# Mixture-of-experts layer on one core: four expert-weight loads under way instead of two, and a block's token slots dealt to the 16 DMA engines in turn

## The chip, the cores and the metric

The kernel runs on one core of one Trainium2 chip. The metric is the device time of one execution in microseconds (us). Work is done by TensorE (PE in the profile, its weight loads PEld), VectorE (DVE), ScalarE (ACT) and GpSimd (POOL). SyncE (SP) issues the plain loads, GpSimd issues the indirect ones, and 16 DMA engines move the data of both.

## The reference, cut to what matters

One layer of a generator is computed for 512 latent tokens of width 1024: two token mixers, then a mixture of experts, then a norm. The change touches the mixture alone.

```python
scores = jax.nn.sigmoid(jnp.matmul(h, w_router, preferred_element_type=jnp.float32))
_, idx = lax.top_k(scores + b_router.astype(jnp.float32), TOP_K)      # 8 of 64 experts a token
wts = jnp.take_along_axis(scores, idx, axis=-1)
wts = (wts / jnp.sum(wts, -1, keepdims=True) * ROUTE_SCALE).astype(h.dtype)
...
def expert_block(acc, blk):
    tok, wt, e = blk
    yb = swiglu(h_pad[tok], w_e_gate[e], w_e_up[e], w_e_down[e]) * wt[:, None]
    return acc.at[tok].add(yb), None
...
return swiglu(h, w_sh_gate, w_sh_up, w_sh_down) + routed[:n]
```

512 tokens with 8 experts each make 4096 (token, expert) pairs. The gate, up and down matrices of an expert are 1024 x 256, 1024 x 256 and 256 x 1024, all float32.

## The kernel before

The mixers, the output projection, the router and the hidden layer of the shared expert fill the first 560 us or so. Then come the experts, in `experts` (L1354), and last a norm of the sum in `tail` (L1558).

**Blocks.** The experts are ranked by their token counts (`rank`), and the rank decides how many slots an expert gets: `CAPS` for the 34 that have a block of 128 partitions to themselves (128, 112, 96 or 80 slots), `PCAPS` for the 30 that share a block two by two (64, 48 or 32 slots, in partitions 0 to 63 and 64 to 127). One more block holds what two large experts have beyond 128. With the two experts of that block, the slots add up to 5376, over 66 slot ranges in 50 blocks. `ORDER` sets the blocks' order: first four single ones, then mostly one pair and two singles in turn, four singles at the end.

**Tables.** For each slot range, `tables` (L1136) compares a row of running numbers (`iot`) with each token's place in its expert's list (`posm`). The result is a one-hot matrix `oh` (four chunks of 128 tokens by 128 slots), and matmuls with it give each slot its token's index and weight. Slot p holds the expert's token number p, so the unused slots are the last ones of the range. An unused slot gets an index out of bounds, whose row is neither read nor written. The tables are made in the background (`background`, L1345), a few blocks ahead of their use.

**A step.** `run` (L1409) works off one block. `fetch` (L1310) gathers the tokens' rows of 4 KB from DRAM by an indirect DMA (`xg<-h2d`), `xpose` turns them, `prep` (L1220) splits each quarter of the weights in two terms (ScalarE writes the first one, VectorE the second, tile `gq`), `mm` multiplies, `act` and `ph` make the hidden layer, `py` (L1279) multiplies by the down matrix. Then an indirect DMA with addition adds the rows into the sum `accd` in DRAM (L1306). A pair has two gathers and two such additions. Since all additions go to one tensor, each waits until the one before has landed. GpSimd issues gathers and additions, in its program order, between multiplications by a gate (L1300).

**Loads of weights.** Each expert has three loads of 1 MB (gate and up in two, down in one) into one of 13 tiles `rw` (`NR`). SP issues them in one order; `pump` issues the next when a tile's last reader has been recorded. `load_part` (L1179) adds one more wait: a load waits until the load `DQ` before it has landed.

```python
self.under_way.append(ins)
if len(self.under_way) > self.DQ:
    self.tc.add_manual_dep(ins.ins, self.under_way[-1 - self.DQ].ins.name, ...
```

There are 195 such loads: 64 experts and the shared one, three each.

Of the kernel before, what the change touches and what calls it, by code (L numbers as in the profile page):

```python
# [12 lines left out]
ALU = mybir.AluOpType  # L13
# [4 lines left out]
P = 128  # L18
# [10 lines left out]
GTYPE = (0, 1, 1, 2)  # L29
NE = 64  # L30
FF = 256

VC_C, VC_CC, VC_NG, VC_ADA = 0, 8, 16, 24
VC_U, VC_TQK, VC_NQ, VC_NK, VC_GA, VC_GB, VC_N = 40, 48, 49, 53, 57, 65, 73
# [39 lines left out]
class Kern:  # L74

    NR, GQ, XB, YB, LQ = 13, 4, 2, 3, 3

    FA, DQ = 2, 2

    TBG, TBN = (1, 2, 4), 12  # L80

# [918 lines left out]
    def shared(self):  # L1000
# [3 lines left out]
        for k in range(KB):  # L1004
            raw = self.raw["sh", k // 4][1].rearrange("p (k f) -> p k f", k=4)[:, k % 4, :]
            w = p1.tile([P, 2, 2 * FF], F32R, name="shw", tag="wlo", bufs=2)
            self.split(w[:, 0, :], w[:, 1, :], raw)
# [4 lines left out]
        for tag in ("sw", f"vals{NE}"):  # L1012
            h = mid.tile([P, 2, FF], F32, name="hs", tag=tag)
            self.hs += [h[:, i, :] for i in range(2)]
        for pg, h in zip(pgs, self.hs):
            sg = p1.tile([P, FF], F32, name="sgs", tag="sgt", bufs=2)
            nc.scalar.activation(sg, pg[:, :FF], AF.Silu)
            nc.vector.tensor_tensor(h, sg, pg[:, FF:], op=ALU.mult)
        self.slots += [self.raw.pop(("sh", n))[0] for n in range(2)]
# [116 lines left out]
    def tables(self, blocks, posm, vals, ps=None):  # L1136

        nc, p2 = self.nc, self.p2
        n = len(blocks)
        pool, tag = (p2, "oh") if ps is None else (self.p1, "sgt")  # L1140
        if ps is None:
            ps = self.ps2.tile([P, n, 6], F32, name="ptab", tag="tab", bufs=1)
        for i, block in enumerate(blocks):
            oh = pool.tile([P, 4, P], BF, name="oh", tag=tag, bufs=2)
            m = P // len(block)
            for p0, (r, t0, _) in zip((0, m), block):
                nc.vector.tensor_tensor(oh[:, :, p0:p0 + m], self.iot[:, None, t0:t0 + m].to_broadcast([P, 4, m]),  # L1147
                                        posm[:, :, r:r + 1].to_broadcast([P, 4, m]), op=ALU.is_equal)
            for b in range(4):
                for p0, (r, _, _) in zip((0, m), block):  # L1150
                    nc.tensor.matmul(ps[p0:p0 + m, i, :], lhsT=oh[:, b, p0:p0 + m], rhs=vals[:, b, r, :],  # L1151
                                     start=b == 0, stop=b == 3)
            yield
        ix, w = self.finish_table(p2 if pool is p2 else self.mid, ps, n)

        half = ix
        if any(len(block) > 1 for block in blocks):
            half = p2.tile([P // 2, n], I32, name="half", tag="half", bufs=self.NTB)
            nc.vector.tensor_copy(half, ix[P // 2:])
        self.tb += [([t[:, i:i + 1] for t in (ix, half)], w[:, i:i + 1]) for i in range(n)]  # L1160
        yield
# [7 lines left out]
    def early(self):  # L1169

        p2 = self.p2
        raw = lambda r: [([P, 2048], F32, f"r{i}") for i in r]
        gq = lambda r: [([P, 2, 2, 2 * FF], F32R, f"gq{i}") for i in r]
        xg = lambda r: [([P, D], F32, f"xg{i}") for i in r]
# [509 lines left out]
```

## Time and profile before

| | us |
|---|---|
| median of three runs | 1391.91 |
| lowest and highest run | 1390.16, 1394.66 |
| the profiled execution, its own time | 1389.76 |
| its span, first to last instruction | 1388.0 |
| PE, DVE, ACT, POOL busy | 1216.1, 905.2, 664.4, 397.8 |

The profiled execution is 1.8 us longer than its span and 2.2 us below the median. Busy times are unions over the whole span; a matmul's own time contains its way through the array, so back-to-back matmuls overlap, and a busy PE may still have room. The DMA share is the time that packets took on the 16 engines; it tells that a packet was under way, not at what speed.

### The profile page before, as it was taken

What the parts mean: (1) busy time and instruction counts of PE and PEld (TensorE: products, weight loads), DVE (VectorE), ACT (ScalarE), POOL (GpSimd) and SP (SyncE); (2) the same over time, 40 slices, a digit from 0 to 9 for tenths busy, and PEclk for the clock granted to TensorE, in tenths of its full rate; (3) what the DMA queues carried; (4) which work ended last, traced back from release to release, by engine and by line L of the source; (5) the groups of instructions that cost most, each with busy time, mean ns of one, the idle gap of its engine ahead of it and who ended that gap; (6) DMA issues with size and microseconds to landing.
All of it is one profiled execution on the core that took longest, in us unless ns stands there. A gap on an engine that the chain in (4) does not pass through costs nothing. (4 is left out here: it accounts for less than half of the span.)

```text
span 1388.0 us, 18578 instructions
## 1 busy us (share of the span) xinstructions
PE 1216.1 (88%) x6305; PEld 862.1 (62%) x6305; DVE 905.2 (65%) x1535; ACT 664.4 (48%) x1146; POOL 397.8 (29%) x374
## 2 busy tenths in 40 slices
PE   6999999999999999898868998787887879777992
PEld 4866887877777788676535555555554546444661
DVE  4536357577687756779958787666665756565653
ACT  4312253365555533355536665555465545454651
POOL 2301103411211000336334343333342333242342
PEclk9999999999999999999988999999998999988996
DMA  9999436655675365857988999999999999999995
GB/s 326 308 295 294 138 114 147 195 141 128 140 155 115 115 211 182 290 201 262 309 276 252 320 296 312 313 306 317 314 313 313 301 330 304 304 327 308 313 328 149
DMA packets 106171, 349.18 MB, mean 252 GB/s; under 512 B 13809, under 2 KB 41050, under 8 KB 81114
## 3 DMA queue, kind: packets, MB, share of 16 engines
q1 hardware_dynamic: 82058, 287.89, 61.0%
q0 software_dynamic: 23552, 58.49, 18.9%
q10 hardware_dynamic: 464, 1.59, 0.3%
q8 instruction: 51, 0.84, 0.2%
q14 instruction: 46, 0.38, 0.1%
HBM read 321.03 MB, written 37.44 MB: 258 GB/s over the span
## 5 line engine op out<-in xcount | busy, mean ns | idle before, releaser
L1229 DVE TENSOR_TENSOR gq<-rw,gq 128x1024 fp32r<-128x1024 f32 x258 | 321.0, 1256 | 132.0 <-ACT gq L1227 130.9
L1243 PE MATMUL pg<-gq,xx 128*128 128x512 f32 x1328 | 401.5, 439 | 3.1 <-DVE gq L1229 1.7
L1227 ACT CAST gq<-rw 128x1024 fp32r<-128x1024 f32 x264 | 273.3, 1046 | 144.8 <-DMA rw<-in_w_exp_dram 91.4
L1243 PEld LDWEIGHTS pg<-gq,xx 128*128 128x128 f32 x1328 | 248.2, 198 | 97.8 <-issue 43.9
L1287 PE MATMUL py<-rw,hT 128*128 128x512 f32 (+1 forms) x560 | 220.1, 633 | 45.0 <-DMA rw<-in_w_exp_dram 41.0
L1287 PEld LDWEIGHTS py<-rw,hT 128*128 128x128 f32 (+1 forms) x560 | 76.4, 175 | 129.7 <-issue 116.8
L1300 POOL TENSOR_TENSOR y<-y,gf 128x512 f32<-128x512 f32 x52 | 82.1, 1579 | 226.9 <-ACT y L1299 226.7
L96 ACT CAST whi<-raw 128x1024 fp32r<-128x1024 f32 (+1 forms) x60 | 61.4, 1023 | 130.4 <-PE mmp L114 43.6
L97 DVE TENSOR_TENSOR wlo<-raw,whi 128x1024 fp32r<-128x1024 f32 (+1 forms) x60 | 71.3, 1189 | 74.9 <-ACT whi L96 74.9
L1306 POOL DMA_INDIRECT accd<-y,ix x50 | 84.5, 1691 | 113.5 <-DVE gq L1229 27.7
L113 PE MATMUL mmp<-hhi,whi 128*128 128x512 f32 x256 | 103.8, 406 | 0.0
L115 PE MATMUL mmp<-hhi,wlo 128*128 128x512 f32 x256 | 101.1, 396 | 0.0
L114 PE MATMUL mmp<-hlo,whi 128*128 128x512 f32 x256 | 100.8, 394 | 0.0
L1319 POOL DMA_INDIRECT xg<-h2d,ix x50 | 58.0, 1161 | 82.3 <-PE xt L1331 51.3
L1331 PE MATMUL xt<-ident,xg 128*128 128x128 f32 x400 | 63.3, 284 | 16.5 <-DMA xg<-h2d,half 15.6
L97 DVE TENSOR_TENSOR xx<-xt,xx 128x512 fp32r<-128x512 f32 x100 | 68.2, 683 | 13.6 <-ACT xx L96 13.2
L1331 PEld LDWEIGHTS xt<-ident,xg 128*128 128x128 f32 x400 | 51.2, 148 | 28.0 <-issue 18.9
L96 ACT CAST xx<-xt 128x512 fp32r<-128x512 f32 x100 | 58.2, 583 | 16.1 <-PE xt L1331 15.3
L762 POOL DMA_DIRECT2D q<-qdr x32 | 17.7, 555 | 144.5 <-PE stp L809 141.9
L1147 DVE TENSOR_TENSOR oh<-iot,posm 128x512 bf16<-128x512 f32 (+1 forms) x66 | 53.3, 835 | 8.2 <-PE ptab L1151 8.2
L1302 DVE SCALAR_TENSOR_TENSOR y<-py,tw,gf 128x512 f32<-128x512 f32 x52 | 38.8, 745 | 30.1 <-PE py L1287 23.7
L113 PEld LDWEIGHTS mmp<-hhi,whi 128*128 128x128 f32 x256 | 48.2, 188 | 12.5 <-issue 3.0
(416 smaller groups left out, 2097.5 us busy)
## 6 DMA issues: line engine op xcount, KB each, us to landing
rw<-in_w_exp_dram SPq DMA_DIRECT2D x195, 1024.0 KB
raw<-in_w_in_dram SPq DMA_DIRECT2D x40, 512.0 KB
araw<-in_w_ada_dram SPq DMA_DIRECT2D x64, 256.0 KB
araw<-in_w_ada_dram SPq DMA_DIRECT2D x16, 512.0 KB
k<-kdr POOLq DMA_DIRECT2D x32, 192.0 KB, 6.1
nab<-in_nab_dram SPq DMA_DIRECT2D x24, 256.0 KB
x<-in_x_dram SPq DMA_DIRECT2D x8, 512.0 KB
q<-qdr POOLq DMA_DIRECT2D x32, 128.0 KB, 5.2
```

The source lines that it names most:

```text
L96: self.nc.scalar.copy(hi, src)
L97: (eng or self.nc.vector).tensor_tensor(lo, src, self.r32(hi), op=ALU.subtract)
L113: mm(ps, lhsT=ahi, rhs=bhi, start=first, stop=False)
L114: mm(ps, lhsT=ahi, rhs=blo, start=False, stop=False)
L115: mm(ps, lhsT=alo, rhs=bhi, start=False, stop=last)
L1227: nc.scalar.copy(t[:, 0, :, sl], src)
L1229: eng.tensor_tensor(t[:, 1, :, sl], src, self.r32(t[:, 0, :, sl]), op=ALU.subtract)
L1243: nc.tensor.matmul(pg, lhsT=st.x[:, q * 2 + k, a, :], rhs=t[:, b, k, :], start=q + k + n == 0, stop=q + k + n == 3 + len(terms))
L1287: nc.tensor.matmul(py[s], lhsT=st.hT[:, j, s], rhs=d[:, j * D + c * 512:j * D + c * 512 + 512], start=j == 0, stop=j == 1)
L1300: nc.gpsimd.tensor_tensor(o, o, gf, op=ALU.mult)
L1306: nc.gpsimd.indirect_dma_start(out=self.accd[:], out_offset=bass.IndirectOffsetOnAxis(ap=ix[:cap], axis=0), in_=y, in_offset=None, bounds_ ...
L1331: self.nc.tensor.transpose(tp[:, k * P:k * P + P], st.xg[:, (q * 4 + k) * P:(q * 4 + k + 1) * P], self.ident)
```

## The change

`DQ` goes from 2 to 4: a weight load now waits for the landing of the fourth load before it. And the slots of a range are filled in another order. With cap slots and k = cap / 16, slot q*k + i holds the expert's token number i*16 + q: sixteen runs of k neighbouring slots, and the tokens are dealt to the runs in turn. Slots beyond the cap, in a block whose range is shorter than its room, are filled by a second comparison.

```diff
+NQ = 16
...
-    FA, DQ = 2, 2
+    FA, DQ = 2, 4
...
-            for p0, (r, t0, _) in zip((0, m), block):
-                nc.vector.tensor_tensor(oh[:, :, p0:p0 + m], self.iot[:, None, t0:t0 + m].to_broadcast([P, 4, m]),
-                                        posm[:, :, r:r + 1].to_broadcast([P, 4, m]), op=ALU.is_equal)
+            for p0, (r, t0, cap) in zip((0, m), block):
+
+                k = cap // NQ
+                nc.vector.tensor_tensor(oh[:, :, p0:p0 + cap].rearrange("p b (q i) -> p b q i", q=NQ),
+                                        self.iot[:, None, t0:t0 + cap].rearrange("p b (i q) -> p b q i", q=NQ)
+                                        .to_broadcast([P, 4, NQ, k]),
+                                        posm[:, :, r:r + 1, None].to_broadcast([P, 4, NQ, k]), op=ALU.is_equal)
+                if cap < m:
+                    nc.vector.tensor_tensor(oh[:, :, p0 + cap:p0 + m],
+                                            self.iot[:, None, t0 + cap:t0 + m].to_broadcast([P, 4, m - cap]),
+                                            posm[:, :, r:r + 1].to_broadcast([P, 4, m - cap]), op=ALU.is_equal)
```

Gathers and additions keep their number and their lists of cap slots. The orders of PE, POOL and SP are the same as before, row for row, but for the waits. On SP, in the middle of the expert loads, four loads stood like this before (the loads raise the semaphores DMAHW0 to DMAHW7 in turn; a load that waits for DMAHW5 raises DMAHW7; the second wait is for the tile's last reader):

```order
L1181 DMA rw_7718<-in_w_exp_dram 128x2048 [waits DMAHW5_49,DVE_49]
L1181 ISA
L1181 DMA rw_7743<-in_w_exp_dram 128x2048 [waits DMAHW6_49,DVE_49]
L1181 ISA
L1181 DMA rw_7781<-in_w_exp_dram 128x2048 [waits DMAHW7_49,DVE_49]
```

The same place on SP now:

```order
L1190 DMA rw_7726<-in_w_exp_dram 128x2048 [waits DMAHW3_49,DVE_49]
L1190 ISA
L1190 DMA rw_7751<-in_w_exp_dram 128x2048 [waits DMAHW4_49,DVE_49]
L1190 ISA
L1190 DMA rw_7789<-in_w_exp_dram 128x2048 [waits DMAHW5_49,DVE_49]
```

Each load waits for a semaphore two places further back; the wait for the tile's reader stays.

On VectorE, among the tables of the first group of eight blocks, there stood before:

```order
L1229 TENSOR_TENSOR gq<-rw,gq 128x1024
L1147 TENSOR_TENSOR oh<-iot,posm_6297 128x512
L1147 TENSOR_TENSOR oh<-iot,posm_6297 128x4x64 x2
L1229 TENSOR_TENSOR gq<-rw,gq 128x1024
L1302 SCALAR_TENSOR_TENSOR y<-py,tw,gf 128x512
```

The same place on VectorE now:

```order
L1238 TENSOR_TENSOR gq<-rw,gq 128x1024
L1150 TENSOR_TENSOR oh<-iot,posm_6297 128x4x112
L1155 TENSOR_TENSOR oh<-iot,posm_6297 128x4x16
L1150 TENSOR_TENSOR oh<-iot,posm_6297 128x4x64 x2
L1238 TENSOR_TENSOR gq<-rw,gq 128x1024
```

A range of 112 slots, which was one comparison over 128, is now one over 112 and one over 16. In all, 66 comparisons become 103: 66 over the caps and 37 over the rest.

## Rows read from the trace of the kernel before

**Rows 1.** The page: span, busy time by engine, and DMA share in 40 slices.

```profile
span 1388.0 us, 18578 instructions
PE 1216.1 (88%) x6305; PEld 862.1 (62%) x6305; DVE 905.2 (65%) x1535; ACT 664.4 (48%) x1146; POOL 397.8 (29%) x374
DMA  9999436655675365857988999999999999999995
```

**Rows 2.** Stretches: length, PE, PEld, DVE, ACT, POOL busy, then clock, DMA share, GB/s.

```profile
560.00:650.00 90.00, 77.53 (x429) 59.32 (x428) 70.61 (x159) 42.14 (x76) 37.50 (x29) 0.94 0.71 245
650.00:1350.00 700.00, 581.83 (x2463) 367.57 (x2461) 478.50 (x568) 377.90 (x519) 257.15 (x176) 0.92 0.96 307
1350.00:1388.00 38.00, 10.60 (x33) 5.50 (x32) 14.33 (x22) 6.08 (x14) 11.51 (x12) 0.70 0.55 170
```

**Rows 3.** Waits of the engines, 650 to 1350: us in total, times, longest.

```profile
ACT gq L1227 <- DMA rw<-in_w_exp_dram: 91.4, 40, 6.2
POOL accd L1306 <- DMA accd<-y,ix: 66.7, 18, 7.9
...
PE py L1287 <- DMA rw<-in_w_exp_dram: 41.0, 7, 7.7
...
POOL accd L1306 <- DMA accd<-y,half: 23.5, 5, 5.3
```

**Rows 4.** Waits of SP's queue, 650 to 1350, the same columns.

```profile
SPq L1181 <- DMA rw<-in_w_exp_dram: 524.1, 170, 7.7
SPq L1181 <- DVE gq L1229: 14.8, 13, 4.0
```

**Rows 5.** DMA, 650 to 1350: packets; queues (packets, MB, share); issues (count, size, us to landing).

```profile
DMA packets 37234, 215.03 MB, mean 307 GB/s; under 512 B 6980, under 2 KB 6980, under 8 KB 15038
q1 hardware_dynamic: 24920, 181.50, 73.3%
q0 software_dynamic: 12272, 33.03, 22.0%
...
rw<-in_w_exp_dram SPq DMA_DIRECT2D x173, 1024.0 KB
accd<-y,ix POOLq DMA_INDIRECT x46, 9.2
xg<-h2d,ix POOLq DMA_INDIRECT x45, 9.5
...
accd<-y,half POOLq DMA_INDIRECT x16, 7.7
xg<-h2d,half POOLq DMA_INDIRECT x15, 10.5
accd<-y,rows POOLq DMA_INDIRECT x3, 8.7
```

**Rows 6.** DMA, 1235 to 1236.4, weight loads alone.

```profile
DMA packets 74, 0.57 MB, mean 404 GB/s; under 512 B 5, under 2 KB 5, under 8 KB 5
q1 hardware_dynamic: 74, 0.57, 97.6%
```

**Rows 7.** DMA, 1238 to 1239, during an addition into accd.

```profile
q0 software_dynamic: 34, 0.14, 75.3%
q1 hardware_dynamic: 9, 0.06, 13.7%
```

**Rows 8.** POOL's timeline, 912 to 928: start, us, instruction, idle before and releaser.

```profile
912.84 1.61 POOL L1306 DMA_INDIRECT accd<-y,ix  x1 [3.29 <-DMA accd<-y,half]
...
925.50 1.57 POOL L1306 DMA_INDIRECT accd<-y,ix  x1 [7.87 <-DMA accd<-y,ix]
```

**Rows 9.** The comparisons of L1147: ns min/median/max, first and last start, forms.

```profile
L1147 DVE TENSOR_TENSOR oh<-iot,posm x66: 403/678/3075, 596.1 to 1078.7; 128x512 bf16<-128x512 f32 x34, 128x256 bf16<-128x256 f32 x32
```

**Rows 10.** VectorE's timeline at 649: one of its small instructions.

```profile
649.00 0.15 DVE L1129 TENSOR_TENSOR ta<-tb 128x2 f32<-128x2 f32 x1
```

**Rows 11.** VectorE's busy time in L1147 alone, 650 to 700.

```profile
650.00:700.00 50.00, 18.99 (x21) 0.97 0.95 306
```

**Rows 12.** VectorE's busy time as a whole, 650 to 700.

```profile
650.00:700.00 50.00, 49.23 (x70) 0.97 0.95 306
```

## Prediction

> **What bounds the kernel now.** The page comes first [rows 1]: PE is busy for 88% of the span, which looks like the bound, but the DMA share stands at 9 tenths nearly throughout the second half. So the stretches come next [rows 2]. From 650 to 1350, half of the span and nearly all of the expert steps, the DMA share is 0.96, PE is busy for only 582 of 700 us, VectorE for 479, ScalarE for 378. From 560 to 650, and after 1350, the DMA engines have room. The change can act on the 700 us.
>
> What the engines wait for there [rows 3]: ScalarE for weights 91.4 us, PE for down matrices 41.0 us. Those 132 us are paid by compute. Why weights come late is read from SP's own queue [rows 4]: of 700 us it waits 524.1 us, 170 times, for the landing of an earlier load, and only 14.8 us for VectorE to give a tile back. So a free tile is nearly always there, and what holds the next load back is the wait on the load two before it.
>
> Then the question is whether the DMA engines could take more, as 0.96 says that they are full. One load moves 1024 KB in packets of 8 KB, 8 for each engine. With weights alone under way, 69 such packets (74 less the 5 small ones) took 97.6% of 16 engines for 1.4 us, 317 ns each, at 404 GB/s [rows 6]. Over the 700 us, 181.50 MB are 22,156 packets of 8 KB, and 73.3% of 16 x 700 us makes 371 ns each, at 307 GB/s with everything [rows 5]. So the share holds 54 ns in each packet that a fed engine doesn't need. And within an addition into accd [rows 7], weights have only 13.7% of the engines, 2 of 16, while the additions have 75.3%, 12 of 16: most engines have done their parts of both loads under way and have no more weights to move until the slowest engine has finished and the next load has come. The 0.96 is not all work.
>
> **The work of the slowest engine.** Weights: 173 loads x 8 packets x 317 ns = 439 us for each engine. The gathers and additions: 15,038 - 6,980 = 8,058 packets of 4 KB [rows 5], 22.0% of 16 x 700 us = 2,464 us of engine time, 306 ns each. 3 of the 125 indirect DMAs carry all 128 rows, so the other 122 carry (8,058 - 384) / 122 = 62.9 rows. Their ranges have 5,376 / 66 = 81.5 slots. If an engine takes cap / 16 neighbouring slots, an engine with early slots has 81.5 / 16 = 5.1 rows each time and one with the last slots none. The front engine's sum: 122 x 5.1 + 3 x 8 = 646 rows, 198 us, in all 637 us. It is at work for 91% of the 700 us, and 63 us are its dry spells.
>
> **The change, part by part.**
>
> *Dealt slots.* Every engine gets 62.9 / 16 = 3.9 rows, rounded up on the front engine, 4.4 on the average: 122 x 4.4 + 24 = 561 rows, 172 us. The slowest engine's work falls to 439 + 172 = 611 us, 26 us less. With no rounding it would be 593 us. If the runs of slots aren't what an engine gets, this part gives 0; no row here tells which engine moves which slot.
>
> *Four under way.* It adds no transfer, it only puts the issue two landings earlier. A load lasts at least 8 x 317 ns = 2.5 us; with two more queued an engine can be 5 us ahead of the slowest and still have weights. Two bounds: all 63 us of dry spells go, or none. Some will stay, since SP's other waits will show up once this one is short: with 13 tiles and four under way, the wait for VectorE, 14.8 us now [rows 4], takes over whenever compute is the slower. I take half, 32 us.
>
> *One-hots.* 66 comparisons of the same elements in all become 103. The 37 more are priced from below by a small instruction, 0.15 us [rows 10], and from above by the shortest half-width comparison, 0.40 us [rows 9]: 6 to 15 us of VectorE. The first operand is now read with steps of 16 elements; no row shows that. The bounds are nothing, and twice the time, 19 us more in 650 to 700 [rows 11]. VectorE is hidden by the DMA wait later (479 of 700 us), but not in 650 to 700, where it is busy for 49.2 of 50 us [rows 12] and feeds the tables that gathers wait for. A third of the comparisons falls there (21 of 66), so some 12 of the 37, 2 to 5 us. I take 3 us, with no price for the steps, and keep 0 to 24.
>
> *What becomes next.* PE's 582 us, VectorE's 479 and the chain of additions. That chain: 46 x 9.2 + 16 x 7.7 + 3 x 8.7 = 573 us from issue to landing [rows 5], each waiting for the one before, as [rows 8] shows in the 7.87 us before 925.50. GpSimd's waits on it are 90 us so far [rows 3]. With 65 x 0.3 us between them it is 592 us, the nearest to 611. So several bounds lie near 600, and a stage with several of them doesn't reach the lowest: another reason for half.
>
> **The sum.** 700 - 26 - 32 + 3 = 645 us for the stretch. The span goes from 1388.0 to 1333 us. With 1.8 us around it, 1334.8; the profiled execution was 2.2 us below the median of the runs shown, so about 1337.
>
> A page has a bound of its own. The Trainium skill, DMA: Bandwidth & Descriptors, section Bandwidth, puts the share of one core in the memory's rate at about 358 GB/s and the fabric at 435. By the first figure the 215.03 MB of the stretch would take at least 601 us, an estimate that leaves the sum as it is; the 404 GB/s over 1.4 us [rows 6] show that the first is no limit for a moment, and no run here shows it for longer.
>
> **The rivals.**
>
> 1. *Packets are slow for another reason.* If the 54 ns are lost in the memory or between two queues on one engine, not in dry spells, the engines are full at 0.96, and only 4% of 700 us, 28 us, is to be had, and dealing out rows takes nothing off. For it: a share of 0.96. Against it: [rows 7]. Half of the 28 us, less the 3 us of comparisons, gives 1381, all of them 1367; I say 1372.
>
> 2. *The slots don't sit in runs.* Then the front engine stays as it is, 637 us plus half of the dry spells is 669, plus 3 us 672: 28 us less, about 1364. Beside it stands a rule: the same page, section The descriptor swizzle, gives each engine of a direct transfer two groups of four partitions, 32 apart. No row shows whether gathers and additions follow it.
>
> 3. *The additions become the bound, and it is slower.* With weights always queued, an addition's row of 354 ns (75.3% of 16 us over 34 packets [rows 7]) has to wait for weight packets of 317 ns on its engine. One a row adds 4.4 x 317 ns = 1.4 us, less 0.7 x 354 ns = 0.2 us for the rows saved: the chain is 592 + 65 x 1.2 = 670 us, and the time at best 1362. With two weight packets for each row it is 592 + 65 x 2.6 = 761 us, 61 us more than now: 1453. It decides from 1.7 us an addition, a median landing of 10.9 us for `accd<-y,ix`. Against it: landings of 9.2 us hold competition already. Beside it stands the page's rule, section Queues, rings and completion order, that an engine takes its queues in turn, packet by packet; that is the lighter case.
>
> 4. *SP is held by tiles instead.* Free tiles now come early [rows 4], but if compute's own order (PE's 582 us) sets the pace, nothing is won beyond small change: 1390.
>
> **Chances.** The forecast 0.56, rival 1 0.18, rival 2 0.10, rival 3 0.09 (half of it in the lighter case), rival 4 0.07. The forecast's own range is 1290 (all dry spells gone and most of the rounding, 598 us) to 1376 (none gone, 26 us less, and 10 us more for the comparisons). The lower end of the whole, 1285, is 593 us for the stretch with the comparisons hidden. The upper end, 1385, takes in rivals 1 and 2 and leaves out rival 4 and the heavy case of 3. 0.3% is 4 us, about the distance between the lowest and the highest run. Faster by more than that: 0.55 + 0.15 + 0.09 + 0.04 = 0.83. Within it: 0.09, most of rival 4 and the weak end of rival 1. Slower: 0.08, the heavy case of rival 3 and comparisons that cost more than twice.
>
> **What would show it.** Right: SP's wait for landings falls from 524 us to below 300, and its waits for VectorE, PE or ScalarE rise; ScalarE's and PE's waits for weights fall from 132 us to below 50; the GB/s of the stretch rise to 330 or more; the mean of an 8 KB packet falls towards 317 ns, or the weights keep their share during an addition. The landing of `accd<-y,ix` stays within 8 to 10 us. If it rises beyond 11 us and GpSimd's waits on accd grow by more than those on weights fall, rival 3 holds. If SP's wait is short, the share is 0.97 and the GB/s are unchanged, it is rival 1. L1150 with L1155 should add 6 to 15 us; 50 us would show that the steps are paid. What makes the prediction wrong above all is that I take half of the dry spells with no row for how the remaining waits add up.

## The result, and the profile after

| | us |
|---|---|
| before, median of four runs (lowest, highest) | 1391.11 (1390.16, 1394.66) |
| changed, median of four runs (lowest, highest) | 1353.98 (1347.73, 1361.02) |
| ratio, 95% interval | 0.973 (0.968 to 0.978) |
| forecast | 1337 (1285 to 1385) |
| profiled execution of the changed kernel, its span | 1361.02, 1359.2 |

Faster by 37 us, where the sum had 55 (26 + 32 - 3). The profiled execution is the slowest of the four, 7 us above the median, and its stretches are longer by that in all. The weights' loads end earlier, and the stretch that was 650 to 1350 is now about 650 to 1320.

The stretches of the changed kernel, columns as in [rows 2]:

```profile
560.00:650.00 90.00, 77.25 (x398) 59.26 (x398) 67.45 (x141) 39.02 (x72) 34.04 (x28) 0.89 0.67 236
650.00:1320.00 670.00, 575.95 (x2487) 368.50 (x2486) 498.33 (x624) 381.41 (x523) 263.55 (x179) 0.94 0.95 325
1320.00:1359.00 39.00, 13.69 (x46) 7.91 (x44) 13.38 (x22) 6.93 (x15) 11.99 (x12) 0.72 0.44 129
```

307 GB/s have become 325, but the DMA share is as high as before: the share alone could not tell that there was room. SP's queue, 650 to 1320 (us, times, longest), answers to [rows 4]:

```profile
SPq L1190 <- DVE gq L1238: 200.3, 61, 8.4
SPq L1190 <- DMA rw<-in_w_exp_dram: 141.0, 75, 4.9
SPq L1190 <- PE py L1296: 90.0, 30, 13.0
SPq L1190 <- DVE hh L1277: 55.3, 15, 17.2
```

The wait for earlier landings fell from 524 to 141 us; SP now waits mostly for tiles that compute has not given back. The other engines in the same stretch, against [rows 3]: what they wait for, and in the last line what is left of the weights. Three waits of the kernel before that [rows 3] leaves out, 650 to 1350, stand ahead of them.

```profile
POOL accd L1306 <- DVE gq L1229: 31.5, 9, 5.2
...
PE ptab L1151 <- DVE oh L1147: 18.5, 8, 9.3
...
PE xt L1331 <- DMA xg<-h2d,half: 15.6, 5, 6.0
```

```profile
POOL accd L1315 <- DMA accd<-y,ix: 65.4, 18, 7.8
...
POOL accd L1315 <- DVE gq L1238: 41.9, 10, 6.8
...
PE xt L1340 <- DMA xg<-h2d,half: 35.5, 9, 7.8
...
POOL accd L1315 <- DMA accd<-y,half: 31.8, 6, 6.7
...
PE ptab L1160 <- DVE oh L1155: 20.3, 9, 13.3
...
ACT gq L1236 <- DMA rw<-in_w_exp_dram: 2.5, 2, 1.7
```

Of 132 us of waits for weights 2.5 are left. PE waits longer for the gather of a pair's second half (35.5 us, 15.6 before). Its 20.3 us for the second comparisons of L1155 are hardly new: the comparisons of L1147 held it for 18.5 us before. The DMA of the stretch, against [rows 5]:

```profile
DMA packets 37769, 217.88 MB, mean 325 GB/s; under 512 B 7066, under 2 KB 7066, under 8 KB 15326
...
q1 hardware_dynamic: 25344, 184.04, 72.1%
q0 software_dynamic: 12382, 33.33, 22.7%
...
accd<-y,ix POOLq DMA_INDIRECT x47, 9.1
...
accd<-y,half POOLq DMA_INDIRECT x16, 8.3
accd<-y,rows POOLq DMA_INDIRECT x3, 8.9
```

The landing of an addition has hardly grown: 9.2 us before and 9.1 now under `ix` (single blocks and the first halves of pairs), 7.7 and 8.3 under `half` (the second halves). The comparisons, 560 to 1359 (busy us, mean ns), beside [rows 9]:

```profile
L1150 DVE TENSOR_TENSOR oh<-iot,posm 128x256 bf16<-128x256 f32 (+6 forms) x66 | 52.0, 800 | 14.3 <-PE ptab L1160 14.3
L1155 DVE TENSOR_TENSOR oh<-iot,posm 128x64 bf16<-128x64 f32 (+2 forms) x37 | 16.4, 444 | 0.0
```

How a late gather comes about, on GpSimd's timeline, 1055 to 1090 (start, us, instruction, idle before it and releaser), and then on PE's:

```profile
1070.43 1.50 POOL L1315 DMA_INDIRECT accd<-y,ix  x1 [6.80 <-DVE gq L1238]
1072.23 1.31 POOL L1328 DMA_INDIRECT xg<-h2d,ix  x1 [0.30 <-DVE oh L1155]
1073.85 1.73 POOL L1328 DMA_INDIRECT xg<-h2d,half  x1 [0.30 <-issue]
1075.88 0.96 POOL L1328 DMA_INDIRECT xg<-h2d,ix  x1 [0.30 <-issue]
```

```profile
1085.00 1.08 PE L1340 MATMUL xt<-ident,xg 128*128 128x128 f32 x4 [4.89 <-DMA xg<-h2d,half]
```

GpSimd stands idle for 6.80 us ahead of an addition; three gathers are queued behind it in GpSimd's order and go out one after the other when it is released; the pair's second half, issued at 1073.85, lets PE start at 1085.00, after 4.89 us of waiting. The profile names VectorE as the releaser. The trace says otherwise: the addition before, issued at 1060.33, landed 9.3 us later, at 1069.6, 0.8 us ahead of this start. All ten additions that the profile puts down to `gq` start 0.78 to 0.81 us after the landing of the one before, as the six named for a half's landing do (0.76 to 0.81); the eighteen named for a landing under `ix` start after 0.27 to 0.82 us. The run `two_acc` below bears it out.

### The profile page after: what moved, and what is told of

It is laid out like the page before. It is cut to its first block, busy times and chain, and to the rows that moved or that the text cites. A ratio compares the mean times of both kernels' runs of the same rounds, so it can differ in the third digit from the quotient of the medians.

```text
span 1359.2 us, 18614 instructions
## 1 busy us (share of the span) xinstructions
PE 1212.7 (89%) x6305; PEld 864.5 (64%) x6305; DVE 921.3 (68%) x1572; ACT 665.2 (49%) x1146; POOL 400.8 (29%) x374
## 5 line engine op out<-in xcount | busy, mean ns | idle before, releaser
L1238 DVE TENSOR_TENSOR gq<-rw,gq 128x1024 fp32r<-128x1024 f32 x258 | 326.5, 1278 | 75.8 <-ACT gq L1236 74.8
L1296 PE MATMUL py<-rw,hT 128*128 128x512 f32 (+1 forms) x560 | 207.5, 605 | 4.6 <-ACT hT L1286 2.5
L1315 POOL DMA_INDIRECT accd<-y,ix x50 | 85.9, 1719 | 145.9 <-DVE gq L1238 41.9
L1296 PEld LDWEIGHTS py<-rw,hT 128*128 128x128 f32 (+1 forms) x560 | 72.3, 167 | 84.6 <-issue 67.6
L1309 POOL TENSOR_TENSOR y<-y,gf 128x512 f32<-128x512 f32 x52 | 78.7, 1514 | 146.9 <-ACT y L1308 146.5
L1340 PE MATMUL xt<-ident,xg 128*128 128x128 f32 x400 | 65.4, 290 | 36.1 <-DMA xg<-h2d,half 35.5
L1150 DVE TENSOR_TENSOR oh<-iot,posm 128x256 bf16<-128x256 f32 (+6 forms) x66 | 52.0, 800 | 14.3 <-PE ptab L1160 14.3
L116 PEld LDWEIGHTS mmp<-hhi,wlo 128*128 128x128 f32 x256 | 48.1, 188 | 10.7 <-issue 0.8
```

What stands on the lines that cost most here:

```text
L116: mm(ps, lhsT=alo, rhs=bhi, start=False, stop=last)
L1238: eng.tensor_tensor(t[:, 1, :, sl], src, self.r32(t[:, 0, :, sl]), op=ALU.subtract)
L1296: nc.tensor.matmul(py[s], lhsT=st.hT[:, j, s], rhs=d[:, j * D + c * 512:j * D + c * 512 + 512], start=j == 0, stop=j == 1)
L1309: nc.gpsimd.tensor_tensor(o, o, gf, op=ALU.mult)
L1315: nc.gpsimd.indirect_dma_start(out=self.accd[:], out_offset=bass.IndirectOffsetOnAxis(ap=ix[:cap], axis=0), in_=y, in_offset=None, bounds_ ...
L1340: self.nc.tensor.transpose(tp[:, k * P:k * P + P], st.xg[:, (q * 4 + k) * P:(q * 4 + k + 1) * P], self.ident)
```

## The experiments

Ratios are to the kernel before, run in the same job; that kernel's median was 1390 to 1396 us in the jobs.

**Each part alone, and more loads.**

`dq4_only` leaves the slots as before, `deal_only` the loads, and `dq8` is the changed kernel with eight loads under way:

```diff
-    FA, DQ = 2, 2
+    FA, DQ = 2, 4      # dq4_only, from the kernel before
-    FA, DQ = 2, 4
+    FA, DQ = 2, 2      # deal_only, from the changed kernel
-    FA, DQ = 2, 4
+    FA, DQ = 2, 8      # dq8, from the changed kernel
```

> Four loads under way, slots as before. By the forecast's sum (the front engine's 637 us of work stay, half of 63 us of dry spells go) it is about 1360 us, 30 us faster than before, and the weights' waits of ScalarE and PE fall as in the changed kernel. If dealing the slots gives nothing, it is the changed kernel's 1354 us or a little less, since it saves 37 comparisons. If the slowest engine sets the pace whatever is queued, it is within 10 us of before (1391 us).

> Dealt slots, two loads under way as before. By the forecast (26 us off the front engine, 3 us for comparisons) about 1368 us. If an engine doesn't get a run of k neighbouring slots, nothing is gained and the comparisons cost 0 to 5 us: 1391 to 1396 us. The first of an addition's 16 landings should come later than before and the last one earlier or the same.

> The changed kernel with eight loads under way. If compute and its tiles are now the bound (SP's waits there are 200 us for VectorE and 90 us for PE beside 141 us for landings), it is within 8 us of the changed kernel's 1354 us. If dry spells remain, it is 10 to 30 us faster. If queued weights slow the gathers and additions, their landings pass 10 us and it is slower than 1360 us.

| | median us | ratio (95%) |
|---|---|---|
| dq4_only | 1361.22 | 0.9735 (0.9695 to 0.9775) |
| deal_only | 1386.76 | 0.9943 (0.9909 to 0.9976) |
| dq8 | 1351.71 | 0.9694 (0.9649 to 0.9740) |

SP's first rows, 650 to 1300, of `dq4_only`, `deal_only` and `dq8`:

```profile
SPq L1181 <- DMA rw<-in_w_exp_dram: 212.6, 87, 4.8
SPq L1181 <- DVE gq L1229: 162.8, 57, 9.9
```

```profile
SPq L1190 <- DMA rw<-in_w_exp_dram: 456.0, 149, 6.2
SPq L1190 <- DVE gq L1238: 27.5, 18, 4.4
```

```profile
SPq L1190 <- DVE gq L1238: 295.5, 72, 13.5
SPq L1190 <- PE py L1296: 89.1, 33, 7.3
SPq L1190 <- DVE hh L1277: 73.6, 14, 16.6
```

Four loads under way alone give as much as both changes, 37 us by the ratio (31 to 43) and 34 between the medians. The dealing alone gives 8 (3 to 13). On top of the four loads it shows nothing (0.973 against 0.9735), but that difference is known to some 9 us only, so 0 and 8 are not told apart. With eight, SP waits for no landing of a load at all, and the time is at most a few us less (the intervals overlap). So something other than the number of loads holds the changed kernel.

Of each gather and addition the trace keeps 16 increments of its semaphore, the 16 landings of the expectation of `deal_only`. They come as it said: from the kernel before to `deal_only` the first one of an addition under `ix` goes from 4.9 to 5.7 us after the issue and the last one from 8.7 to 8.4; of a gather under `ix`, from 5.0 to 6.0 and from 9.9 to 9.4 (means after 650 us, where the trace tells the increments of one transfer from those of the next). From `dq4_only` to the changed kernel the same four move the same way: 5.7 to 6.3 and 8.9 to 8.7, 5.0 to 5.9 and 10.1 to 9.3. So the dealing evens the landings out, but the last one comes only 0.2 to 0.8 us earlier.

**Fewer second comparisons, by full slots.** Every expert gets 128 or 64 slots, so of the 37 second comparisons only the two in the block of what lies beyond 128 stay:

```diff
-CAPS = [128] * 13 + [112] * 6 + [96] * 7 + [80] * 8
-PCAPS = [64] * 16 + [48] * 11 + [32] * 3
+CAPS = [128] * 34
+PCAPS = [64] * 30
```

> The changed kernel with every range as wide as its room (128 or 64 slots), so that 35 of the 37 second comparisons go and the lists of slots get longer, the added slots all unused. If the comparisons on VectorE cost time (16 us in all, part of it while PE waits for tables), it is 3 to 10 us faster than 1354 us. If the longer lists cost GpSimd and the queues more, it is slower by as much. Within 3 us: neither is on the path.

Measured: 1387.43 us, 0.9943 (0.9907 to 0.9978), so 30 us slower than the changed kernel. The slots rise from 5376 to 6352, and all 976 new ones are unused. Its additions and PE's wait, 650 to 1300:

```profile
accd<-y,ix POOLq DMA_INDIRECT x44, 10.4
...
accd<-y,half POOLq DMA_INDIRECT x15, 7.1
```

```profile
PE xt L1340 <- DMA xg<-h2d,half: 48.3, 9, 8.2
```

An addition under `ix` lands in 10.4 us, where the changed kernel has 9.3 in the same stretch, but a pair's second half in 7.1 instead of 8.3, and gathers land earlier too (medians of 7.2 and 7.7 us instead of 9.1 and 9.8). PE's wait for a pair's gather grows from 35.5 to 48.3 us. What costs the 30 us stays open, with two candidates. One is the longer lists themselves: each unused slot still sends small packets, as the last section shows. The other is that the dealing fails on full ranges. The 16 landings of a gather of 128 slots come in two halves here, the eighth at 5.5 us and the ninth at 9.0 on average (64 slots: 6.6 and 8.8), while ranges of 80 and 96 slots in the changed kernel show no such gap (7.9 and 7.9, 8.2 and 8.3). As a test of the comparisons the run says nothing, since it made something else worse; `trim` does that.

**What holds the changed kernel.** Four edits of it. `trim` leaves the second comparisons out and multiplies over cap columns:

```diff
+            nc.vector.memset(ps, 0.0)
...
-                if cap < m:
-                    nc.vector.tensor_tensor(oh[:, :, p0 + cap:p0 + m], ...
...
-                    nc.tensor.matmul(ps[p0:p0 + m, i, :], lhsT=oh[:, b, p0:p0 + m], rhs=vals[:, b, r, :],
+                    nc.tensor.matmul(ps[p0:p0 + cap, i, :], lhsT=oh[:, b, p0:p0 + cap], rhs=vals[:, b, r, :],
```

> The changed kernel, with the tables cut to the slots that an expert's block has: the second comparison of a block (for the slots beyond its cap) is left out, the four products go over cap columns, and the table's PSUM tile is set to zero first. The addresses and weights that are used stay the same. Theory: the 37 second comparisons (16.4 us of VectorE, for which PE's table products waited 20 us in 9 places) stand on the path, so the changed kernel would get 10 to 16 us faster: a ratio of 0.962 to 0.966 to the kernel before, and PE's waits for the line 1155 are gone. Rival: they lie beside the other waits of those steps (gathers, additions), and leaving them out is worth under 4 us: 0.970 to 0.974.

`two_acc` halves the chain of additions: every second one goes to a tensor that nobody reads, so half of the experts' output is left out of the result.

```diff
+                self.nacc += 1
+                acc = self.accd if self.nacc % 2 else self.acc2
-                nc.gpsimd.indirect_dma_start(out=self.accd[:], ...
+                nc.gpsimd.indirect_dma_start(out=acc[:], ...
```

> The changed kernel, with every second addition going to another DRAM tensor, which nobody reads: half of the experts' output is left out of the result. An addition then waits for the landing of the one before the last, not of the last. Theory: in the changed kernel, the additions that wait for landings on GpSimd (65 us for whole blocks' and 32 us for halves' landings between 650 and 1320 us) hold up the gathers of the pairs queued behind them, and these hold PE (36 us in 9 waits for a half's gather). Then these waits go and the kernel is 20 to 35 us faster than the changed one: a ratio of 0.948 to 0.959. Rival: the gathers are late because there are only two tiles to gather into, which come free when PE has transposed the last one; then the waits of GpSimd move to the transposes, PE's waits for a half's gather stay near 36 us, and the time stays within 6 us of the changed kernel's: 0.969 to 0.977.

`nr12` and `nr12_x3`, a third tile to gather into and its control:

```diff
-    NR, GQ, XB, YB, LQ = 13, 4, 2, 3, 3
+    NR, GQ, XB, YB, LQ = 12, 4, 2, 3, 3      # nr12
+    NR, GQ, XB, YB, LQ = 12, 4, 3, 3, 3      # nr12_x3
-    FA, DQ = 2, 4
+    FA, DQ = 3, 4                            # nr12_x3
```

> The changed kernel with 12 tiles of weights instead of 13: a control for the next run, which needs the room. Theory that loads no longer bound the time in most of the stretch: 0 to 10 us slower than the changed kernel, a ratio of 0.973 to 0.980, with SP's waits for readers of a tile up. Rival, that each tile of loads in advance still counts: one of thirteen, over 15 us slower, 0.984 or more.

> As the run with 12 tiles of weights, with a third tile to gather into, and gathers issued three blocks ahead instead of two. Theory that the pairs' gathers are late because of the two tiles: PE's waits for a half's gather (36 us in 9) go under 10 us, and the kernel is 15 to 35 us faster than the control with 12 tiles. Rival, that they are late because GpSimd issues them behind additions that wait for landings: an issue a block earlier still clears them, since it is ahead of one more addition; so a gain here alone doesn't settle it, but no gain (within 5 us) with the waits for gathers gone would say that PE's waits only move elsewhere, to the weights or to the tables.

| | median us | ratio (95%) |
|---|---|---|
| trim | 1358.37 | 0.9729 (0.9697 to 0.9760) |
| two_acc | 1327.83 | 0.9514 (0.9483 to 0.9545) |
| nr12 | 1355.41 | 0.9715 (0.9683 to 0.9748) |
| nr12_x3 | 1346.35 | 0.9646 (0.9615 to 0.9676) |

`two_acc` is the one that moves the time, by 2.2% or 30 us of the changed kernel. GpSimd's groups in it, 650 to 1300 (busy us, mean ns, idle before and releasers):

```profile
L1319 POOL DMA_INDIRECT accd<-y,ix x33 | 59.0, 1787 | 15.7 <-POOL y L1311 7.8 <-DVE pos L1495 6.8 <-DVE oh L1157 0.6
...
L1319 POOL DMA_INDIRECT acc<-y,ix x16 | 32.4, 2025 | 4.5 <-POOL y L1311 4.2 <-DVE oh L1157 0.3
L1319 POOL DMA_INDIRECT acc<-y,half x16 | 23.3, 1457 | 4.9 <-issue 4.9
```

and PE's transposes and SP's first wait:

```profile
L1344 PE MATMUL xt<-ident,xg 128*128 128x128 f32 x376 | 57.3, 275 | 3.4 <-DMA xg<-h2d,half 3.4
```

```profile
SPq L1192 <- DMA rw<-in_w_exp_dram: 352.5, 133, 5.0
```

The additions wait for next to nothing; the waits that the profile had put down to `gq` went with those named landings, as the 0.8 us above had it. PE's wait for gathers falls from 35.5 to 3.4 us with the same two tiles to gather into, which throws out the rival. SP waits for landings of loads again: the loads bind. In the profiled executions nearly all of the gain is made before 1000 us: from 650 to 1000 PE is busy for 312 us instead of 291, from 1000 to 1250 for 220 instead of 218, and there both kernels move 359 GB/s. So the chain costs its time early.

`nr12_x3` takes 9 us against its control, less than forecast, though PE waits for no gather any more. GpSimd and PE in it, 650 to 1300:

```profile
POOL accd L1315 <- DMA accd<-y,ix: 119.5, 21, 8.4
```

```profile
PE ph L1282 <- DVE hh L1277: 36.5, 14, 14.0
```

Earlier gathers get past the additions, but the chain is as long as it was: GpSimd's waits on it rise (119.5 us, 65.4 in the changed kernel), and PE waits elsewhere (36.5 us, 24.2 there). One weight tile less costs nothing (`nr12`, where SP's waits for landings stay at 132 us of 650). And `trim`: the 16.4 us of second comparisons are worth nothing measurable, the rival was right.

**With the additions out of the way.** `two_acc_nat` is `two_acc` with the slots as before the change, and leaves out the same half. `two_sum` uses both sums, so that nothing is left out; `two_sum_dq8` and `two_sum_trim` add eight loads under way, and `trim`'s edit:

```diff
+                if st.b is not None:
+                    nc.gpsimd.dma_start(self.acc2[st.b * P:st.b * P + P], y)
+                    self.nsh += 1
+                    continue
+                self.nacc += self.nsh == 4
+                acc = self.acc2 if self.nacc % 2 else self.accd
...
                 nc.sync.dma_start(a[:, c], self.accd[bs, c])
+                nc.sync.dma_start(t[:, c], self.acc2[bs, c])
+                nc.vector.tensor_tensor(a[:, c], a[:, c], t[:, c], op=ALU.add)
```

> The run with every second addition going to a tensor that nobody reads (half of the experts' output left out), without the dealing of slots: four loads under way alone. With the additions' chain out of the way, SP waits again for landings of weights (352 us in 133 waits between 650 and 1300 us). Theory: the dealing is worth little on top of four loads only because the additions hide it; where loads bind again, the 26 us of work that it takes off the fullest DMA engine show, at least 10 us of them: 1338 to 1354 us, a ratio of 0.958 to 0.970 against 0.951 with the dealing. Rival: the fullest engine's work is not what sets the rate of the loads, and the dealing is worth under 5 us here too: 0.948 to 0.955.

> The changed kernel with two accumulators that are both used: the shared expert's four blocks are written to the second one as plain rows, later the experts' additions go to the one and the other in turn, and the end reads both and sums them (2 MB more to read and four additions of 128x1024 on VectorE). Nothing is left out of the result. Theory: the 29 us that the additions' chain cost the changed kernel come back, less 6 to 10 us at the end and what the first blocks still wait: 1332 to 1340 us, a ratio of 0.954 to 0.960. Rival: the end costs as much as the chain did: 0.968 or more.

> The same with eight loads under way. Theory that loads bind once the additions are out of the way, through dry spells that four loads leave: 5 to 15 us faster than with four. Rival, that what is left of SP's waits for landings is the rate that 16 engines give (349 GB/s in the last 300 us): within 4 us of four loads.

> The version with two accumulators that are both used (four loads under way), with the tables cut to the slots that a block has, as in the run that left the second comparisons out. There they were worth nothing, but the additions' chain stood beside them. Theory: they were hidden by the chain, and PE's 20 us of waits for comparisons between 650 and 1300 us (16 us of it for the second ones) are on the path now: 8 to 16 us faster than with them, a ratio of 0.950 to 0.956. Rival: PE waits for weights instead (25 us now), since SP's loads run at 346 GB/s whatever PE does: within 4 us of the version with them, 0.959 to 0.965.

| | median us | ratio (95%) |
|---|---|---|
| two_acc_nat | 1332.93 | 0.9573 (0.9544 to 0.9602) |
| two_sum | 1341.75 | 0.9620 (0.9588 to 0.9652) |
| two_sum_dq8 | 1336.61 | 0.9583 (0.9555 to 0.9612) |
| two_sum_trim | 1340.53 | 0.9631 (0.9591 to 0.9671) |

The dealing is worth 0.0059 of 1395.9, or 8 us (2 to 14 by the intervals), where loads bind: between the theory (10 or more) and the rival (under 5), and neither is thrown out. Where it gains and loses is in the stretches of `two_acc_nat` and then of `two_acc` (the last number is GB/s):

```profile
650.00:740.00 90.00, 78.45 (x385) 47.45 (x384) 80.17 (x115) 48.57 (x66) 46.08 (x29) 0.94 0.96 318
740.00:1000.00 260.00, 231.32 (x1025) 146.40 (x1023) 198.84 (x238) 160.41 (x219) 110.33 (x74) 0.97 0.99 333
1000.00:1250.00 250.00, 213.34 (x887) 136.04 (x888) 171.33 (x193) 146.98 (x201) 96.85 (x65) 0.95 1.00 349
```

```profile
650.00:740.00 90.00, 75.77 (x360) 44.65 (x358) 79.35 (x122) 43.23 (x58) 47.23 (x27) 0.91 0.91 287
740.00:1000.00 260.00, 236.30 (x1050) 151.05 (x1046) 206.45 (x266) 164.99 (x225) 117.17 (x76) 0.97 0.99 339
1000.00:1250.00 250.00, 220.02 (x925) 140.27 (x925) 179.54 (x207) 150.68 (x207) 96.37 (x67) 0.95 1.02 359
```

From 1000 to 1250 the dealing adds 10 GB/s, 2.9%; from 650 to 740, while the tables are made, 31 GB/s are missing. The other two pairs have the same signs: 281 to 272 early and 314 to 320 late with two loads under way, 288 to 271 and 348 to 359 with four. So the late gain is the same 10 or 11 GB/s with the whole chain and with half of it.

`two_sum` is the fastest kind that leaves nothing out, and `two_sum_dq8`, at 0.958 the best of them, beats the changed kernel by 1.5%. Its gain over `two_sum` is inside the intervals. `two_sum` missed its theory's range: it keeps half of the 30 us. In the profiled executions 8 us lie behind the steps (spans of 1333.2 and 1325.2 us, the waits from 650 to 1300 as in `two_acc`), for reading and adding the second sum; the rest of the 14 us between the medians is not accounted for. `two_sum_trim` is no faster than `two_sum`: the comparisons stay hidden with the chain gone too.

## Why the prediction was right, and where it was off

**The bound, and four under way: right.** SP's wait for the load two before was what held the loads. Forecast 32 us from half of the dry spells, measured 37 (`dq4_only`). The half was taken without a row for it, as the prediction says itself, so the nearness is in part luck: SP's other waits did take over, as it said, but behind them stood the chain of additions. What it named as signs came: the wait for landings 141 us (below 300 asked), waits for weights 2.5 us (below 50), landings of additions under `ix` 9.1 us (8 to 10). GB/s are 325 over the stretch, where 330 were asked, and 359 from 1000 to 1250.

**Dealt slots, 26 us: the term that failed.** Measured 8 alone, 8 with the chain halved, and nothing clear of the noise on top of four loads. The step that failed is that the front engine's saved work is taken off the stretch in full. The runs show that the dealing loses early what it gains later; the late gain, 2.9%, is near the 4% of the sum (637 to 611 us). Why the loads go slower from 650 to 740 stays open. The second comparisons are not the cause as far as runs show: `trim`, without them, has the changed kernel's 271 GB/s there. That the additions hide what is saved is not shown: the late gain is there with the whole chain too. A further share may be lost on the 29 of 66 ranges that have 128 or 64 slots, if the halves of `fullcaps` mean that such a range isn't dealt evenly; no run tests it.

**The price of a packet, 317 ns: not reached, and no floor.** 184.04 MB are 22,466 packets of 8 KB, and 72.1% of 16 x 670 us makes 344 ns each, half of the way from 371. The 404 GB/s of [rows 6] held for a moment only. At 344 ns, 173 x 8 packets are 476 us for an engine instead of 439, and the floor of 611 us would be 648. But from 1000 to 1250 the share of the changed kernel is 1.01 and that of `two_acc` 1.02, so the recorded times of packets overlap and do not add up to an engine's work. At the 359 GB/s that held there, the stretch's 217.88 MB would take 607 us, an estimate close to the 611.

**One-hots, 3 us: small and hidden.** 52.0 + 16.4 us against 53 before, 15 us more, the top of the 6 to 15. Of them at most 7 us are for reading with steps: the 52.0 us are for 5376 slots, where 6400 took 53.3 before, 44.8 for as many. In time the second comparisons are worth nothing measurable (`trim`, `two_sum_trim`).

**What becomes next: named, not priced.** The chain of additions was put at 592 us, as the nearest bound. It is now 47 x 9.1 + 16 x 8.3 + 3 x 8.9 + 66 x 0.3 = 607 of 670 us, and costs 30 us without filling the stretch. The sum took it for a floor that matters only once everything else is under it. But a chain with little slack does damage at each place where two additions come close: it delays the gathers behind it. The prediction also took only the rows named as landings for the chain's waits (90 us); those named for `gq`, 31.5 us before and 41.9 in the changed kernel, were landings too.

**The rivals.** (1) Not so: GB/s rose from 314 to 359 late, at shares of 0.96 and 1.01; the packets' recorded time, though, fell only half of the way. (2) Not so for most ranges: the dealing changes the rate late, and the first of 16 landings comes later and the last one earlier. For 128 slots the rule beside this rival would give the halves of `fullcaps`, with the first four slots of a run of eight on one engine and the last four on another; no view shows which engine moves which slot. (3) Half right: the additions became the bound, but not by clearly slower landings, and the result was a smaller gain, not a loss. (4) SP is held by tiles now, 200 us for VectorE, but behind the gain and not instead of it.

The loads alone measured 37 us and the two changes together 37, which leaves about nothing, give or take 9 us, for the dealing less its comparisons, where the sum had 23.

## What to carry to other kernels

Before a term is added to a sum, ask which bound stands next and how much slack it has in each step, not only over the stretch: here eight loads under way gave nothing over four, while a chain of additions at 90% of the stretch already cost 30 us. A wait that a queue keeps on an earlier transfer can be tested by one number, how many are under way; when doubling it again changes neither the rate nor the time, stop. Read all of an instruction's waits together, since the profile put some landings down to VectorE; the time from the last landing to the start tells them.

## What the runs showed of the hardware

**A plateau of the loads.** With the additions halved and the loads binding again, eight under way do no more than four. From 1000 to 1250, SP's first wait in `two_acc` (four), the rate there, and SP's first wait in `two_sum_dq8` (eight; its rate in that stretch is 362 GB/s):

```profile
SPq L1192 <- DMA rw<-in_w_exp_dram: 190.6, 73, 4.7
```

```profile
DMA packets 15117, 89.85 MB, mean 359 GB/s; under 512 B 2700, under 2 KB 2700, under 8 KB 5615
```

```profile
SPq L1192 <- DMA rw<-in_w_exp_dram: 189.3, 73, 4.6
```

The same wait and rate with twice the loads queued (`two_sum` itself, with four, has 190.7 us and 360 GB/s; the changed kernel and `dq8` have 359 and 363 GB/s): some 360 GB/s is what this mix of loads, gathers and additions gives here, over 250 us. The Trainium skill, DMA: Bandwidth & Descriptors, section Bandwidth, has about 358 GB/s as one core's share of the memory, reached with both cores of a memory domain streaming, and measures 425 for 16 MB transfers of a core alone. The kernel here has one core at work and still stays at the first figure; no stretch of this length came near the second.

**Unused slots.** The packets of the whole execution, first in the changed kernel and then in `fullcaps`:

```profile
DMA packets 106170, 349.17 MB, mean 257 GB/s; under 512 B 13809, under 2 KB 41050, under 8 KB 81114
```

```profile
DMA packets 108123, 349.19 MB, mean 253 GB/s; under 512 B 15761, under 2 KB 43002, under 8 KB 83066
```

976 more unused slots send 1,952 more packets of under 512 B, two for each; of larger ones there is one more in 92,000. So no row is moved for an unused slot, but it is not nothing to the queue either. What share of the 30 us they have, against the two halves of the landings, no run separates.
